# Attention scores of two heads in row groups of 64, value products next to the scores, and two moves in the gated recurrence

## The chip, the core and the metric

The kernel runs on one core of one Trainium2 chip. TensorE (PE) multiplies matrices; "PEld" is its weight load. VectorE (DVE), ScalarE (ACT) and GpSimd (POOL) do the elementwise work, SyncE (SP) issues the DMAs. The metric is the device time of one execution in microseconds; the median of several runs is given.

## The reference, cut to what matters

One layer of a hybrid streaming encoder: 1024 tokens of width 1024. A normed input is projected to a gated recurrence with four heads of 128 (branch a), a band attention with eight heads of 64 (branch b), and two gates; the branches are merged, then follow a feed-forward part and a last gated addition. The change lies in the two token mixers:

```python
def band_attention(q, k, v, qn_g, kn_g, rel_bias):
    # each chunk of 64 tokens attends to itself and the previous 8 chunks
    qh = head_rms(q, qn_g); kh = head_rms(k, kn_g)
    scores = einsum('bnqhd,bnkhd->bnhqk', qc, kb) * 64 ** -0.5
    probs = softmax(where(valid, scores + bias, -1e30))
    return einsum('bnhqk,bnkhd->bnqhd', probs, vb)

# recurrence, per chunk and head: qt, kt, it are q, k and value, b the summed log decay
    o = (qt * exp(b)) @ state + attn @ it
    state = exp(b_last) * state + (kt * exp(b_last - b)).T @ it
# then o = head_rms(o, onorm_g) * silu(g)
```

## The kernel before, in words

Weights and activations are split into a high and a low part in a rounded 32-bit format (fp32r); a product of two split numbers is three matmuls, high by high, high by low and low by high. Everything that must keep its order is chained by hand: each matmul (`mul`, L84) and each transpose (`tr`, L87) in the order in which the code issues it, so too the DMAs on SP and the operations that go through the wrappers `self.V`, `self.A` and `self.G` (shown as L55). Operations called on `nc.scalar` or `nc.gpsimd` directly are placed by a scheduler. PSUM tiles (`pm`) come from a pool of single banks of 128 x 512.

**Recurrence** (`hgrn_mix`, L558 on; about 372 to 536.8 us). For each of four heads, levels m = 1, 2, 4 to 64 build the scores within blocks of 128 tokens; then the keys are transposed in two halves (copied by ACT, L625), and eight blocks follow one another: a state product `pk`, the two products of the output `po`, an update of the state on DVE. A finished half's squares and its power are made (ACT L652, POOL L653 and L654); its scaling `hgrn_gate` (ACT L663) and its transposed output `hgrn_out` come later, among the levels of the next head. Each `yield` hands over to the "fill", here `attn_in`: the projection of q and k for the attention, in pieces of matmuls with weights that POOL (`wl`, L130) and ACT (`wh`, L124) split. `attn_in` squares and sums each block's q and k (power on POOL, L729 and L730), scales them on DVE and stores them with two strided DMAs, each value twice.

**Attention** (`attention`, L877 on; 536.8 to 703 us). Four pairs of heads times eight query blocks of 128 are 32 steps, and two more to drain; the second pair lies between 579.78 and 619.64 us. A query block sees up to five key blocks. For step n the code issues: the scores of head 0; the transposes of the next step's q and k (`attn_stack`: four of 128 x 128, since each head's q and k lie there twice, one copy above the other); the scores of head 1; one piece of feed work (two in the first three steps); the transposed probabilities of step n−1 (`attn_pt`, ten transposes in a full step, and the reciprocal sums spread over 64 columns); the value products of step n−2 (`attn_pv`, the two heads in the two column halves of the array); another piece of feed. Feed are matmuls of branch a and of gates, three per piece. ACT stores the query as [high; low] on 128 rows and the keys as high and remainder (`k1`, `k2`, two slots each), each key twice; so one head's scores are two matmuls over 128 rows for each of one or two groups of key blocks (`attn_scores`). DVE makes the low parts (`scalar_tensor_tensor`), adds the bias and takes the row minimum of the negated scores; ACT takes the exponential.

Of the kernel before, what the change touches and what calls it, by code (L numbers as in the profile page):

```python
# [11 lines left out]
F32R = mybir.dt.float32r  # L12
U32 = mybir.dt.uint32
AF = mybir.ActivationFunctionType
ALU = mybir.AluOpType
AX = mybir.AxisListType

P = 128
# [24 lines left out]
def f32(ap):  # L43
    return ap.bitcast(F32)
# [13 lines left out]
class Trunk:  # L58
# [493 lines left out]
    def hgrn_mix(self, h):  # L552
# [20 lines left out]
        while m < P:  # L573
            nb = T // m
            qv = q[:, :].rearrange("p (j two m) -> p j two m", two=2, m=m)
            kv = kt[:, :].rearrange("p (j two m) -> p j two m", two=2, m=m)
            per = 64 // m
            ps = sums(2) if m == 1 else self.mm()
            for c in range(8):
                if 1 < m < 32:  # L580
                    some = 16 // m
                    for j in range(4):
                        b = c * per + j * some
                        self.mul(
                            ps[32 * j:32 * j + 32, 16 * c:16 * c + 16], kt[:, c * P + 32 * j:c * P + 32 * j + 32],
                            qv[:, b:b + some, 1, :], start=True, stop=True)
                elif m >= 32:
                    for j in range(per):
                        self.mul(ps[2 * m * j:2 * m * j + m, c * m:c * m + m], kv[:, c * per + j, 0, :], qv[:, c * per + j, 1, :], start=True, stop=True)
            tv = cur.rearrange("p (j two) -> p j two", two=2)  # L590
            self.V.tensor_tensor(qv[:, :, 1, :], qv[:, :, 1, :], tv[:, :, 0:1].to_broadcast([P, nb // 2, m]), ALU.mult)
            self.V.tensor_tensor(kv[:, :, 0, :], kv[:, :, 0, :], tv[:, :, 1:2].to_broadcast([P, nb // 2, m]), ALU.mult)
            nxt = tt[:, at_col:at_col + nb // 2]
            at_col += nb // 2
            self.V.tensor_tensor(nxt, tv[:, :, 0], tv[:, :, 1], ALU.mult)
            av = at[:, :].rearrange("p (c j two m) -> p c j two m", c=8, two=2, m=m)[:, :, :, 1, :]
            if 1 < m < 32:
                some = 16 // m
                for j in range(4):
                    rows, b = slice(32 * j, 32 * j + 32), j * some  # L600
                    mk = self.masks[rows, LEVELS.index(m), 16 * j:16 * j + 16].rearrange("p (j m) -> p j m", m=m).unsqueeze(1).to_broadcast([32, 8, some, m])
                    self.V.copy_predicated(av[rows, :, b:b + some, :], mk, ps[rows, :P].rearrange("p (c j m) -> p c j m", c=8, m=m))
            elif m == 1:
                mk = self.masks[:, LEVELS.index(m), :].rearrange("p (j m) -> p j m", m=m).unsqueeze(1).to_broadcast([P, 8, per, m])
                self.V.copy_predicated(av, mk, ps[:, :].rearrange("p (c j m) -> p c j m", c=8, m=m))
            else:
                for j in range(per):
                    rows = slice(2 * m * j, 2 * m * j + m)
                    (self.V.tensor_copy if j == 0 else nc.scalar.copy)(av[rows, :, j, :], ps[rows, :8 * m].rearrange("p (c m) -> p c m", m=m))
            cur = nxt  # L610
            yield 1900 if m == 1 else 2400 if m < 32 else 1400 if m == 32 else 2000
            if m == 1:
                yield from self.hgrn_out()
            if m == 2:
                self.hgrn_gate()
            if m == 4:
                yield from self.hgrn_out()
            m *= 2

        ktok = self.slot()  # L620
        for i in range(2):
            ps = self.mm()
            for c in range(4):
                self.tr(ps[:, c * P:c * P + P], kt[:, i * HALF + c * P:i * HALF + c * P + P], self.eye)
            nc.scalar.copy(ktok[:, i * HALF:i * HALF + HALF], ps)  # L625
            yield 600
        if self.oa[h] is None:
            self.oa[h] = self.slot()
        for c in range(8):
            cs = slice(c * P, c * P + P)  # L630
            if c % 4 == 0:
                po = self.mm()
            if c < 7:
                pk = self.mm()
                self.mul(pk[:, :P], ktok[:, cs], v[:, cs], start=True, stop=True)
            o = po[:, (c % 4) * P:(c % 4) * P + P]
            self.mul(o, at[:, cs], v[:, cs], start=True, stop=c == 0)
            if c:
                self.mul(o, q[:, cs], state, start=False, stop=True)
            if c == 0:  # L640
                self.V.tensor_copy(state, pk[:, :P])
            elif c < 7:
                self.V.scalar_tensor_tensor(state, state, cur[:, c:c + 1], pk[:, :P], ALU.mult, ALU.add)
            yield 450
            if c == 6:
# [59 lines left out]
        self.G.tensor_scalar(bt, bt, -1.0, None, ALU.mult)  # L705

    def attn_keys(self):
        self.k1 = [self.slot(F32R) for _ in range(2)]
        self.k2 = [self.slot(F32R) for _ in range(2)]

    def attn_values(self):
        self.v = [self.slot() for _ in range(4)]
# [3 lines left out]
    def attn_in(self):  # L716
# [15 lines left out]
        def scale():  # L732
            g, b, ps, ss, _ = late.pop(0)
            t = self.small(HALF, tag="qo")
            self.V.tensor_tensor(
                t[:, :].rearrange("p (a d) -> p a d", d=64), ps[:, :].rearrange("p (a d) -> p a d", d=64),
                ss[:, :].unsqueeze(2).to_broadcast([P, 8, 64]), ALU.mult)
            to = self.qd[g, b] = self.spill()
            for i in range(2):
                self.store(  # L740
                    to[:, :].rearrange("p (a two d) -> p a two d", two=2, d=64)[:, :, i, :], t[:, :].rearrange("p (a d) -> p a d", d=64))

        for g in range(2):
            gates = iter(range(len(CHUNKS) - len(PLAIN) + g, len(CHUNKS), 2))
# [51 lines left out]

    def attn_load(self, pair, b):
        qk = self.qk[pair, b] = self.small(HALF, tag="qk")
        self.load(qk, self.qd[pair // 2, b][:, pair % 2 * HALF:pair % 2 * HALF + HALF])

    def attn_stack(self, pair, b):

        qk = self.qk.pop((pair, b))
        ps = self.mm()
        for a in range(4):
            self.tr(ps[:, a * P:a * P + P], qk[:, a * P:a * P + P], self.eye)
        q = self.qs[pair, b] = self.small(256, F32R, tag="qs")
        c = slice(b % 4 * 256, b % 4 * 256 + 256)
        k1, k2 = self.k1[b // 4][:, c], self.k2[b // 4][:, c]
        gk = self.cols[:, C_GK:C_GK + 1]  # L810
        self.A.activation(k1, ps[:, 256:512], AF.Copy, scale=gk)
        self.A.activation(q, ps[:, 0:256], AF.Copy, scale=self.gq8[:, 0:1])
        yield
        self.V.scalar_tensor_tensor(k2, ps[:, 256:512], gk, f32(k1), ALU.mult, ALU.subtract)
        lo = q[64:128, :]
        self.V.scalar_tensor_tensor(lo, ps[64:128, 0:256], self.gq8[64:128, 0:1], f32(lo), ALU.mult, ALU.subtract)

    def attn_scores(self, pair, b, h):

        k0 = max(0, b - 4)  # L820
        nb = b + 1 - k0
        bias = self.bias[pair, h]
        q = self.qs[pair, b][:, h * P:h * P + P]
        s = self.small(640, tag="s")
        mn = self.small(2, tag="mx2")
        last = None
        for i in range(2):
            lo, hi = max(k0, 4 * i), min(b + 1, 4 * i + 4)
            if hi <= lo:
                continue  # L830
            ps = self.mm()[:, :(hi - lo) * P]
            for j, k in enumerate((self.k1[i], self.k2[i])):
                keys = k[:, :].rearrange("p (b two t) -> p b two t", two=2, t=P)[:, lo - 4 * i:hi - 4 * i, h, :]
                self.mul(ps, q, keys, start=j == 0, stop=j == 1)
            c = slice((lo - k0) * P, (hi - k0) * P)
            e = slice(640 + (lo - b - 1) * P, 640 + (hi - b - 1) * P)
            init = 3.0e38 if last is None else last
            self.V.tensor_tensor_reduce(s[:, c], ps, bias[:, e], 1.0, init, ALU.add, ALU.min, mn[:, i:i + 1])
            last = mn[:, i:i + 1]
        return s[:, :nb * P], last  # L840

# [30 lines left out]
    def attention(self, fill):  # L872
# [1 line left out]
        steps = [(p, b) for p in range(4) for b in range(8)]  # L874
        whole = len(steps)
        feed = chain(fill, self.branch_a())
        sc, dens, pts = {}, {}, {}  # L877

        def stack(n):
            if n >= whole:  # L880
# [3 lines left out]
                self.bias_load(p + 1, b == 5)  # L884
            return self.attn_stack(p, b)

        def scores(n, h):
            if n < whole:
                sc[n, h] = self.attn_scores(*steps[n], h)

        def exp(n, h):
            if n < whole:
# [4 lines left out]
        def norm(n):  # L897
            if 0 <= n < whole:
                self.V.reciprocal(dens[n], dens[n])
# [15 lines left out]
        for n in range(whole + 2):  # L915
            if n < whole and steps[n][1] == 0:
                self.ob.append(self.slot())
            norm(n - 1)
            scores(n, 0)
            st = stack(n + 1)  # L920
            next(st, None)
# [2 lines left out]
            exp(n, 0)  # L924
            drain(st)
            scores(n, 1)
            for _ in range(2 if n < 3 else 1):
                next(feed, None)
            pt(n - 1, 0)
            pt(n - 1, 1)  # L930
# [9 lines left out]
                self.scale()  # L940
            if n > 3:
                next(item, None)
            next(feed, None)
        drain(feed)

    def branch_src(self):
# [1013 lines left out]
```

## Time and profile before

| | us |
|---|---|
| median of 3 runs | 1590.02 |
| lowest and highest | 1587.98 and 1591.01 |
| the profiled execution's own time | 1587.8 |
| its span, first to last instruction | 1586.0 |
| PE busy in it | 1554.9 (98%) |
| DVE busy | 1165.6 (73%) |
| POOL busy | 724.0 (46%) |
| ACT busy | 613.0 (39%) |

The mean clock granted to TensorE was 0.998 of full speed. Busy times of matmuls overlap, since a matmul starts while the one before it still drains; from one start to the next is what a matmul takes of PE's time. A row of a timeline gives the start and the length in us, the engine, line and operation, the tiles written and read (buffer numbers left out), the array's part used (rows x columns), and how many like it follow one another; in square brackets stands the idle time before it and the engine that ended it.

### The profile page before, as it was taken

How to read it: one execution, taken by the hardware profiler on the slowest of the kernel's cores; microseconds unless marked ns; L12 is line 12 of the kernel's file. 1: busy time of each engine (PE TensorE's matmuls, PEld its weight loads, DVE VectorE, ACT ScalarE, POOL GpSimd, SP SyncE). 2: the span in 40 equal slices, each digit the busy share in tenths (PEclk: the TensorE clock that was granted, in tenths of full speed). 3: DMA queues.
4: the chain of work that ended last, by engine and by line, in shares of the span. 5: the costliest groups of instructions: out<-in, count | busy, mean ns of one | idle time of the engine just before them, and what ended most of it. 6: DMA issues, size and time to landing. Idle time of an engine off the chain costs nothing. (4 is left out here: it accounts for less than half of the span.)

```text
span 1586.0 us, 22842 instructions
## 1 busy us (share of the span) xinstructions
PE 1554.9 (98%) x8708; PEld 1275.0 (80%) x8708; DVE 1165.6 (73%) x1582; ACT 613.0 (39%) x1033; POOL 724.0 (46%) x459
## 2 busy tenths in 40 slices
PE   8999999999989999999999999999999999999998
PEld 6888877887767788888888788888888887888887
DVE  8748787847887577766888888888888757438653
ACT  6332233332323566652567222222222235337321
POOL 4213342244545711106213677777777756446420
PEclk9999999999999999999999999999999999999999
DMA  5326666461542765444345323333233287655521
GB/s 192 133 94 227 241 208 219 160 221 66 167 135 55 238 201 171 171 157 175 107 157 185 118 100 109 101 108 104 100 100 100 73 302 272 215 178 178 196 73 53
DMA packets 125085, 244.22 MB, mean 154 GB/s; under 512 B 42800, under 2 KB 51504, under 8 KB 124208
## 3 DMA queue, kind: packets, MB, share of 16 engines
q1 hardware_dynamic: 124832, 242.75, 44.6%
q8 instruction: 68, 1.11, 0.3%
q14 instruction: 41, 0.34, 0.1%
q10 hardware_dynamic: 144, 0.02, 0.0%
HBM read 166.97 MB, written 75.76 MB: 153 GB/s over the span
## 5 line engine op out<-in xcount | busy, mean ns | idle before, releaser
L84 PE MATMUL pm<-s,whi 128*128 128x512 f32 x1808 | 563.9, 393 | 2.7 <-DVE t L55 2.4
L84 PE MATMUL pm<-s,wh 128*128 128x512 f32 (+1 forms) x1496 | 464.4, 392 | 2.2 <-DVE s L55 2.0
L84 PEld LDWEIGHTS pm<-s,whi 128*128 128x128 f32 x1808 | 339.3, 188 | 81.0 <-DVE t L55 3.2
L84 PE MATMUL pm<-s,wlo 128*128 128x512 f32 x904 | 355.2, 393 | 0.0
L130 POOL TENSOR_TENSOR wl<-wr,wh 128x1024 fp32r<-128x1024 f32 (+2 forms) x114 | 225.1, 1989 | 247.5 <-ACT wh L124 245.0
L55 DVE TENSOR_TENSOR s<-s,s 128x512 f32<-128x512 f32 (+3 forms) x249 | 285.6, 1168 | 61.1 <-ACT s L55 42.6
L84 PEld LDWEIGHTS pm<-s,wh 128*128 128x128 f32 x1496 | 275.8, 188 | 61.6 <-issue 5.5
L84 PE MATMUL pm<-s,wl 128*128 128x512 f32 (+1 forms) x748 | 290.4, 388 | 1.3 <-POOL wl L130 1.3
L84 PEld LDWEIGHTS pm<-s,wlo 128*128 128x128 f32 x904 | 169.8, 188 | 39.3 <-DVE wlo L55 0.2
L55 DVE TENSOR_TENSOR t<-pm,t 128x512 f32<-128x512 f32 x166 | 114.0, 687 | 93.0 <-PE pm L84 86.3
L84 PE MATMUL pm<-wh,s 128*128 128x512 f32 x512 | 171.1, 401 | 5.3 <-ACT wh L124 5.3
L84 PEld LDWEIGHTS pm<-s,wl 128*128 128x128 f32 x748 | 140.8, 188 | 30.8 <-POOL wl L130 1.7
L124 ACT CAST wh<-wr 128x1024 fp32r<-128x1024 f32 (+1 forms) x91 | 91.6, 1008 | 179.8 <-PE pm L84 90.0
L55 POOL TENSOR_TENSOR wlo<-wr,whi 128x512 fp32r<-128x512 f32 (+1 forms) x62 | 115.9, 1877 | 84.1 <-ACT whi L55 82.7
L55 DVE TENSOR_TENSOR s<-pm,s 128x512 f32<-128x512 f32 x117 | 77.4, 687 | 90.9 <-PE pm L84 87.5
L84 PEld LDWEIGHTS pm<-wh,s 128*128 128x128 f32 x512 | 97.1, 190 | 25.3 <-ACT wh L124 5.3
L55 POOL TENSOR_TENSOR s<-s,t 128x512 f32<-128x512 f32 x44 | 76.9, 1748 | 88.6 <-ACT t L55 88.6
L55 ACT CAST whi<-q 128x512 fp32r<-128x512 f32 (+1 forms) x63 | 47.8, 759 | 151.0 <-DVE q L55 130.5
L84 PE MATMUL pm<-wl,s 128*128 128x512 f32 x256 | 100.9, 394 | 1.2 <-POOL wl L130 1.2
L55 ACT CAST s<-s 128x1024 fp32r<-128x1024 f32 x76 | 75.7, 1009 | 46.5 <-DMA s<-d 23.4
L55 POOL TENSOR_TENSOR wlo<-q,whi 128x512 fp32r<-128x512 f32 x41 | 70.5, 1718 | 14.4 <-ACT whi L55 14.4
L55 ACT ACTIVATE t<-s 128x512 f32<-128x512 f32 x44 | 27.9, 634 | 123.0 <-DVE s L55 119.5
(148 smaller groups left out, 1970.9 us busy)
## 6 DMA issues: line engine op xcount, KB each, us to landing
s<-d SPq DMA_DIRECT2D x79, 512.0 KB, 5.6
d<-s SPq DMA_DIRECT2D x123, 256.0 KB, 2.9
wr<-d SPq DMA_DIRECT2D x28, 512.0 KB, 3.6
d<-t SPq DMA_DIRECT2D x54, 256.0 KB, 2.6
wr<-in_sg SPq DMA_DIRECT2D x22, 512.0 KB, 4.0
wr<-in_su SPq DMA_DIRECT2D x22, 512.0 KB, 4.3
d<-m SPq DMA_DIRECT2D x40, 256.0 KB, 3.7
m<-d SPq DMA_DIRECT2D x32, 256.0 KB, 3.4
```

Source lines behind the costliest of these rows:

```text
L55: return lambda *a, **k: self.trunk.order(op(*a, **k), self.key)
L84: return self.order(self.nc.tensor.matmul(*a, **k))
L124: self.nc.scalar.copy(hi[:, c], raw[:, c])
L130: rest.tensor_tensor(lo[:, c], raw[:, c], f32(hi[:, c]), ALU.subtract)
```

## The change

1. **Scores.** q and k are stored once, in one contiguous store per block, and loaded 256 columns wide. `attn_stack` makes two transposes: head 0's 64 features land on rows 0 to 63, head 1's on rows 64 to 127. Query and keys are split into high and low for both heads at once, with the keys in one slot each for `k1` and `k2`. A new function `attn_products` issues for each group of key blocks (up to four, or three and two when there are five) three products per head (high·high, high·low, low·high), head 0 on rows 0 to 63 and head 1 on rows 64 to 127 alternating, each head in a PSUM bank of its own; a step with five key blocks takes four banks.
2. **Order.** `products(n)` stands at the start of step n, right behind the value products of the step before; all feed pieces of the step stand in its middle.
3. **Recurrence, gating.** `hgrn_gate` comes behind level 4 instead of level 2, the second `hgrn_out` behind level 16 instead of level 4.
4. **Recurrence, state.** The first state product and its copy to `state` come right behind the transposes of the second half of the keys, without a fill piece between; they need the first half only.

```diff
-            if m == 2:
+            if m == 4:
                 self.hgrn_gate()
-            if m == 4:
+            if m == 16:
                 yield from self.hgrn_out()
...
             nc.scalar.copy(ktok[:, i * HALF:i * HALF + HALF], ps)
+            if i:
+                pk = self.mm()
+                self.mul(pk[:, :P], ktok[:, :P], v[:, :P], start=True, stop=True)
+                self.V.tensor_copy(state, pk[:, :P])
             yield 600
...
-            if c < 7:
+            if 0 < c < 7:
                 pk = self.mm()
...
-            if c == 0:
-                self.V.tensor_copy(state, pk[:, :P])
-            elif c < 7:
+            if 0 < c < 7:
                 self.V.scalar_tensor_tensor(state, state, cur[:, c:c + 1], pk[:, :P], ALU.mult, ALU.add)
...
-        self.k1 = [self.slot(F32R) for _ in range(2)]
-        self.k2 = [self.slot(F32R) for _ in range(2)]
+        self.k1, self.k2 = self.slot(F32R), self.slot(F32R)
...
-            for i in range(2):
-                self.store(
-                    to[:, :].rearrange("p (a two d) -> p a two d", two=2, d=64)[:, :, i, :], t[:, :].rearrange("p (a d) -> p a d", d=64))
+            self.store(to[:, :HALF], t)
...
-        for a in range(4):
+        for a in range(2):
             self.tr(ps[:, a * P:a * P + P], qk[:, a * P:a * P + P], self.eye)
...
-        self.A.activation(k1, ps[:, 256:512], AF.Copy, scale=gk)
-        self.A.activation(q, ps[:, 0:256], AF.Copy, scale=self.gq8[:, 0:1])
+        self.A.activation(k1, ps[:, P:2 * P], AF.Copy, scale=gk)
+        self.A.activation(q1, ps[:, :P], AF.Copy, scale=gq)
         yield
-        self.V.scalar_tensor_tensor(k2, ps[:, 256:512], gk, f32(k1), ALU.mult, ALU.subtract)
-        lo = q[64:128, :]
-        self.V.scalar_tensor_tensor(lo, ps[64:128, 0:256], self.gq8[64:128, 0:1], f32(lo), ALU.mult, ALU.subtract)
-
-    def attn_scores(self, pair, b, h):
+        self.V.scalar_tensor_tensor(k2, ps[:, P:2 * P], gk, f32(k1), ALU.mult, ALU.subtract)
+        self.V.scalar_tensor_tensor(q2, ps[:, :P], gq, f32(q1), ALU.mult, ALU.subtract)
+
+    def attn_products(self, pair, b):
...
+        q = self.qs.pop((pair, b))
+        cuts = [0, nb] if nb < 5 else [0, 3, nb]
+        parts = [[], []]
+        for lo, hi in zip(cuts, cuts[1:]):
+            c = slice((k0 + lo) * P, (k0 + hi) * P)
+            ps = [self.mm()[:, :(hi - lo) * P] for _ in range(2)]
+            for j, (qs, ks) in enumerate(((q[:, :P], self.k1), (q[:, :P], self.k2), (q[:, P:], self.k1))):
+                for h in range(2):
+                    rows = slice(64 * h, 64 * h + 64)
+                    self.mul(ps[h], qs[rows, :], ks[rows, c], start=j == 0, stop=j == 2)
+            for h in range(2):
+                parts[h].append((lo, hi, ps[h]))
+        return nb, parts
...
-            ps = self.mm()[:, :(hi - lo) * P]
-            for j, k in enumerate((self.k1[i], self.k2[i])):
-                keys = k[:, :].rearrange("p (b two t) -> p b two t", two=2, t=P)[:, lo - 4 * i:hi - 4 * i, h, :]
-                self.mul(ps, q, keys, start=j == 0, stop=j == 1)
...
             norm(n - 1)
+            products(n)
             scores(n, 0)
...
-            for _ in range(2 if n < 3 else 1):
+            for _ in range(3 if n < 3 else 2):
                 next(feed, None)
...
-            next(feed, None)
```

PE, a step with four key blocks in the second pair, before: the row of the value products' end (tile `m` by `s`, 64 wide), the feed piece (tiles `wh`, `wl`), then the scores of head 0, four transposes, the scores of head 1 and the feed again.

```order
L84 MATMUL pm_5685<-m_5611,s_4944 64x128 x2
L84 MATMUL pm_5669<-s_4596,wh_4915 128x512
L84 MATMUL pm_5669<-s_4597,wh_4915 128x512
L84 MATMUL pm_5669<-s_4596,wl_4914 128x512
L84 MATMUL pm_5699<-s_4860,m_5654 128x512
L84 MATMUL pm_5699<-s_4862,m_5654 128x512
L87 MATMUL pm_5703<-eye,m_5446 128x128 x4
L84 MATMUL pm_5719<-s_4860,m_5654 128x512
L84 MATMUL pm_5719<-s_4862,m_5654 128x512
L84 MATMUL pm_5669<-s_4702,wh_4915 128x512
```

The same place now (`s_4848` is k1, `s_4849` is k2, the two `pm` are the two heads' banks):

```order
L84 MATMUL pm_5113<-m_5053,s_4927 64x128 x2
L84 MATMUL pm_5118<-s_4848,m_5076 128x512
L84 MATMUL pm_5119<-s_4848,m_5076 128x512
L84 MATMUL pm_5118<-s_4849,m_5076 128x512
L84 MATMUL pm_5119<-s_4849,m_5076 128x512
L84 MATMUL pm_5118<-s_4848,m_5076 128x512
L84 MATMUL pm_5119<-s_4848,m_5076 128x512
L87 MATMUL pm_5129<-eye,m_4925 128x128 x2
L84 MATMUL pm_5094<-s_4692,wh_4878 128x512
L84 MATMUL pm_5094<-s_4693,wh_4878 128x512
```

The feed piece has gone from between the value products and the scores; six products in one piece stand where four in two pieces stood.

PE in the recurrence, end of head 0's transposes (tiles `eye`), as the difference between the two kernels; `s_2621` holds the values, `s_3172` the transposed keys:

```order
 L87 MATMUL pm_3173<-eye,s_2708 128x128 x4
 L87 MATMUL pm_3179<-eye,s_2708 128x128 x4
+L84 MATMUL pm_3185<-s_2621,s_3172 128x128
 L84 MATMUL pm_3131<-wh_2614,s_256 128x512
 L84 MATMUL pm_3131<-wl_2613,s_256 128x512
```

The first state product is now ahead of the fill piece that stood between it and the transposes.

POOL between heads 1 and 2, before: powers of two q/k blocks (L729, L730), two weight pieces (L130) and the power of a finished half (L653, L654).

```order
L729 TENSOR_TENSOR m_3805<-m_3805,mhalf 128x8
L730 TENSOR_SCALAR m_3805<-m_3805,m_464 128x8
L130 TENSOR_TENSOR wl_3730<-wr_3732,wh_3731 128x256 x4
L729 TENSOR_TENSOR m_3808<-m_3808,mhalf 128x8
L730 TENSOR_SCALAR m_3808<-m_3808,m_464 128x8
L130 TENSOR_TENSOR wl_3794<-wr_3796,wh_3795 128x256 x4
L653 TENSOR_SCALAR m_3849<-m_3849 128x4
L654 TENSOR_TENSOR m_3849<-m_3849,mhalf 128x4
```

And now:

```order
L130 TENSOR_TENSOR wl_3727<-wr_3729,wh_3728 128x256 x4
L130 TENSOR_TENSOR wl_3788<-wr_3790,wh_3789 128x256 x4
L730 TENSOR_TENSOR m_3799<-m_3799,mhalf 128x8
L731 TENSOR_SCALAR m_3799<-m_3799,m_464 128x8
L730 TENSOR_TENSOR m_3802<-m_3802,mhalf 128x8
L731 TENSOR_SCALAR m_3802<-m_3802,m_464 128x8
L655 TENSOR_SCALAR m_3843<-m_3843 128x4
L656 TENSOR_TENSOR m_3843<-m_3843,mhalf 128x4
```

Both weight pieces have moved ahead of the powers of the q/k blocks; the half's power is last in both.

More of the change, by code (lines that the diff above doesn't have):

```diff
@@ L798, in attn_load @@
         qk = self.qk[pair, b] = self.small(HALF, tag="qk")
-        self.load(qk, self.qd[pair // 2, b][:, pair % 2 * HALF:pair % 2 * HALF + HALF])
+        self.load(qk[:, :256], self.qd[pair // 2, b][:, pair % 2 * 256:pair % 2 * 256 + 256])
     def attn_stack(self, pair, b):
@@ L804, in attn_stack, with attn_scores @@
         ps = self.mm()
-        for a in range(4):
+        for a in range(2):
             self.tr(ps[:, a * P:a * P + P], qk[:, a * P:a * P + P], self.eye)
         q = self.qs[pair, b] = self.small(256, F32R, tag="qs")
-        c = slice(b % 4 * 256, b % 4 * 256 + 256)
-        k1, k2 = self.k1[b // 4][:, c], self.k2[b // 4][:, c]
-        gk = self.cols[:, C_GK:C_GK + 1]
-        self.A.activation(k1, ps[:, 256:512], AF.Copy, scale=gk)
-        self.A.activation(q, ps[:, 0:256], AF.Copy, scale=self.gq8[:, 0:1])
+        c = slice(b * P, b * P + P)
+        k1, k2, q1, q2 = self.k1[:, c], self.k2[:, c], q[:, :P], q[:, P:]
+        gk, gq = self.cols[:, C_GK:C_GK + 1], self.gq8[:, 0:1]
+        self.A.activation(k1, ps[:, P:2 * P], AF.Copy, scale=gk)
+        self.A.activation(q1, ps[:, :P], AF.Copy, scale=gq)
         yield
-        self.V.scalar_tensor_tensor(k2, ps[:, 256:512], gk, f32(k1), ALU.mult, ALU.subtract)
-        lo = q[64:128, :]
-        self.V.scalar_tensor_tensor(lo, ps[64:128, 0:256], self.gq8[64:128, 0:1], f32(lo), ALU.mult, ALU.subtract)
-    def attn_scores(self, pair, b, h):
+        self.V.scalar_tensor_tensor(k2, ps[:, P:2 * P], gk, f32(k1), ALU.mult, ALU.subtract)
+        self.V.scalar_tensor_tensor(q2, ps[:, :P], gq, f32(q1), ALU.mult, ALU.subtract)
+    def attn_products(self, pair, b):
         k0 = max(0, b - 4)
         nb = b + 1 - k0
+        q = self.qs.pop((pair, b))
[11 more added lines that the diff above has]
+        return nb, parts
+    def attn_scores(self, pair, nb, parts, h):
         bias = self.bias[pair, h]
-        q = self.qs[pair, b][:, h * P:h * P + P]
         s = self.small(640, tag="s")
@@ L826, in attn_scores @@
         last = None
[L827 to L830, printed above, removed]
-            ps = self.mm()[:, :(hi - lo) * P]
-            for j, k in enumerate((self.k1[i], self.k2[i])):
-                keys = k[:, :].rearrange("p (b two t) -> p b two t", two=2, t=P)[:, lo - 4 * i:hi - 4 * i, h, :]
-                self.mul(ps, q, keys, start=j == 0, stop=j == 1)
-            c = slice((lo - k0) * P, (hi - k0) * P)
-            e = slice(640 + (lo - b - 1) * P, 640 + (hi - b - 1) * P)
+        for i, (lo, hi, ps) in enumerate(parts[h]):
+            e = slice(640 + (lo - nb) * P, 640 + (hi - nb) * P)
             init = 3.0e38 if last is None else last
-            self.V.tensor_tensor_reduce(s[:, c], ps, bias[:, e], 1.0, init, ALU.add, ALU.min, mn[:, i:i + 1])
+            self.V.tensor_tensor_reduce(s[:, lo * P:hi * P], ps, bias[:, e], 1.0, init, ALU.add, ALU.min, mn[:, i:i + 1])
             last = mn[:, i:i + 1]
@@ L876, in attention @@
         feed = chain(fill, self.branch_a())
-        sc, dens, pts = {}, {}, {}
+        sc, dens, pts, prods = {}, {}, {}, {}
         def stack(n):
@@ L885, in stack, with products @@
             return self.attn_stack(p, b)
+        def products(n):
+            if n < whole:
+                prods[n] = self.attn_products(*steps[n])
         def scores(n, h):
             if n < whole:
-                sc[n, h] = self.attn_scores(*steps[n], h)
+                sc[n, h] = self.attn_scores(steps[n][0], *prods[n], h)
         def exp(n, h):
```

## The prediction

> **What bounds the kernel now.** I read the page first, then the waits of TensorE (PE), then busy time by stage, then a timeline of one attention step. The page's span and its row of busy times (busy us, share of the span, instructions):
>
> ```profile
> span 1586.0 us, 22842 instructions
> PE 1554.9 (98%) x8708; PEld 1275.0 (80%) x8708; DVE 1165.6 (73%) x1582; ACT 613.0 (39%) x1033; POOL 724.0 (46%) x459
> ```
>
> PE is the bound: 31 us of the span is left idle. Four of its waits lie where the change works (us in total, times, longest):
>
> ```profile
> PE pm L84 <- ACT m L663: 4.8, 2, 4.1
> PE pm L84 <- DVE s L55: 4.5, 8, 1.3
> PE pm L84 <- POOL wl L130: 2.5, 3, 1.3
> PE pm L84 <- DVE state L55: 1.7, 2, 0.9
> ```
>
> Busy time in the gated recurrence (372 to 536.8), in the attention, and in the attention's second head pair alone (window: length, busy us of PE, weight loads, DVE, ACT, POOL, granted clock, DMA share, GB/s):
>
> ```profile
> 372.00:536.80 164.80, 155.49 (x1716) 125.63 (x1715) 119.72 (x237) 54.30 (x152) 87.09 (x91) 0.99 0.38 112
> 536.80:703.00 166.20, 164.19 (x1378) 138.94 (x1377) 128.14 (x384) 113.78 (x273) 34.34 (x37) 1.00 0.55 179
> 579.78:619.64 39.86, 39.86 (x341) 33.96 (x340) 31.30 (x96) 27.30 (x67) 6.40 (x6) 1.00 0.55 182
> ```
>
> In the second pair PE works for 39.86 of 39.86 us. So a PE instruction taken out of the attention is time gained, as long as DVE, 31.30 us busy, stays below. Its last step, PE's timeline (start, us until the last one's end, instructions grouped):
>
> ```profile
> 613.69 0.86 PE L84 MATMUL pm<-s,m 128*128 128x128 f32 x4
> 614.38 0.60 PE L87 MATMUL pm<-eye,m 128*128 128x128 f32 x4
> 614.74 0.93 PE L84 MATMUL pm<-s,m 128*128 128x128 f32 x4
> 615.51 0.62 PE L84 MATMUL pm<-s,wh 128*128 128x512 f32 x2
> 615.97 0.39 PE L84 MATMUL pm<-s,wl 128*128 128x512 f32 x1
> 616.20 1.25 PE L87 MATMUL pm<-eye,m 128*128 128x128 f32 x10
> 617.38 0.44 PE L84 MATMUL pm<-eye,m 128*64 128x128 f32 x4
> 617.65 1.26 PE L84 MATMUL pm<-m,s 128*64 128x128 f32 x20
> 618.84 0.73 PE L84 MATMUL pm<-s,wh 128*128 128x512 f32 x2
> 619.40 0.40 PE L84 MATMUL pm<-s,wl 128*128 128x512 f32 x1
> 619.64 0.33 PE L84 MATMUL pm<-s,m 128*128 128x128 f32 x2
> ```
>
> The busy times overlap; what counts is start to start. The step takes 619.64 − 613.69 = 5.95 us: scores of head 0 (.69), four transposes (.36), scores of head 1 (.77), three feed products of 512 columns (.69, so .23 each), ten transposes (1.18), 24 half-width matmuls (1.46), three feed products (.80).
>
> **The scores.** The 16 score blocks of the second pair, from one's start to the next instruction's (window: length, PE busy); first, last and sum:
>
> ```profile
> 579.78:579.95 0.17, 0.17 (x3) 1.00 0.00 0
> ...
> 614.74:615.51 0.77, 0.77 (x8) 1.00 0.00 0
> ...
> sum 8.09, PE 8.09; mean PE 0.51
> ```
>
> Removed: 8.09 × 4 pairs = 32.4 us. Removed too: two of four transposes in each of 32 steps, at about .10 (.36/4 = .09, 1.18/10 = .118): 6.4 us.
>
> Added: per cut three products for each head, the two heads in different halves of the array's rows. If both run at once, a pair costs what one costs: 512 columns .23, in proportion .17 for 384 and .115 for 256, and about .11 for 128, where the next weights set the pace as in the transposes. Eight steps: one block 3 × .11 = .33; two 3 × .115 = .345; three 3 × .17 = .51; four 3 × .23 = .69; then four steps of five blocks, 3 × .17 + 3 × .115 = .858 each, 3.43. Sum 5.31, × 4 = 21.2 us. It is 144 pairs in all (3, 3, 3, 3 and 4 × 6, times four).
>
> No row shows two row halves at once. The nearest are two column halves, in a timeline of 0.1 us:
>
> ```profile
> 617.65 0.28 PE L84 MATMUL pm<-m,s 128*64 128x128 f32 x2
> ```
>
> and their group in the second pair (busy us, mean ns of one, idle before):
>
> ```profile
> L84 PE MATMUL pm<-m,s 128*64 128x128 f32 x120 | 7.9, 273 | 0.0
> ```
>
> Two that take .273 each are over within .28, so the second started some .007 behind the first. Bounds for the row halves: full overlap, 21.2, and none, 42.5; I take the first, the row it is nearest to.
>
> **The array's mode.** The order on PE becomes: products (row halves), transposes and feed (whole array), transposes, sums and value products (column halves), then the next products. That is three changes of shape a step where there were two. From 616.20 to 619.64 the trace shows a round trip, whole to columns to whole: 3.44 us, against 10 × .10 + 12 column pairs × .11 + 3 × .23 = 3.01 without changes, so .43 at that reckoning and .35 if a transpose is .109. I take .18 for one change: 32 × .18 = 5.8 us, bounds 0 and .35 × 32 = 11.2. The Trainium skill, page "TensorEngine Tiling (Array Packing)", Key Properties, says that changing the tiling mode, and not merely the tile, drains the TensorE. By that rule products directly behind value products pay such a drain and the term stands; were it false here, the term would be 0 and the sum 5.8 lower. The round trip agrees with the rule, and no row shows column to row.
>
> The feed products keep their number and their 512 columns; three of six change places: nothing. They ask for their weights 1.18 + 1.46 = 2.6 us earlier in the step; if those came late it would cost such a wait as the three of PE for POOL wl above, 2.5/3 = .8 each, but in the second pair PE never waited for them.
>
> **DVE.** Its rows in the second pair (busy us, mean ns, idle before):
>
> ```profile
> L55 DVE SCALAR_TENSOR_TENSOR m<-pm,gq,m 64x256 fp32r<-64x256 f32 x8 | 3.9, 491 | 0.1
> L55 DVE SCALAR_TENSOR_TENSOR s<-pm,cols,s 128x256 fp32r<-128x256 f32 x8 | 3.9, 484 | 3.8 <-ACT m L55 3.7
> ...
> L55 DVE TENSOR_TENSOR s<-pm,m 128x128 f32<-128x128 f32 x8 | 2.3, 291 | 1.3 <-PE pm L84 1.2
> ```
>
> Both subtractions become 128 wide: by the last row .29 instead of .49 and .48, 8 × .39 = 3.1 us less of 31.3. PE's pair falls by 11.8/4 = 2.95 to 36.9, so DVE is 28.2/36.9 = 76% busy. The next products wait for this step's subtractions and for free banks, the reductions of head 1 among them; ahead of them on PE stand the six feed products, ten transposes and 24 half-width matmuls, 1.4 + 1.2 + 1.5 = 4.1 us, and all of DVE's work of a step is 28.2/8 = 3.5. That hides it; without the cover the cost is the rival below.
>
> **DMA.** Stores and loads of q and k (KB each, us to landing):
>
> ```profile
> d<-m SPq DMA_DIRECT2D x40, 256.0 KB, 3.7
> m<-d SPq DMA_DIRECT2D x32, 256.0 KB, 3.4
> ```
>
> Loads halve and the paired strided stores become one. SP issues a load five steps (some 25 us) ahead of its use: nothing gained.
>
> **The recurrence.** The first state product is now straight behind the second half's transposes and needs ACT's copy of the first half. Transposes and copies of heads 1 and 3, and where PE went on:
>
> ```profile
> 426.16 1.03 PE L87 MATMUL pm<-eye,s 128*128 128x128 f32 x8
> 426.95 0.48 PE L84 MATMUL pm<-wh,s 128*128 128x512 f32 x1
> 427.20 0.59 ACT L625 COPY s<-pm 128x512 f32<-128x512 f32 x1
> 516.62 1.03 PE L87 MATMUL pm<-eye,s 128*128 128x128 f32 x8
> 517.31 1.08 ACT L625 COPY s<-pm 128x512 f32<-128x512 f32 x2 [3.77 <-PE pm L87]
> ```
>
> PE could go on .79 after the first transpose: at 426.95 and 517.41. The first copies end at 427.79 and 517.31 + .54 = 517.85. So a new wait of .84 where ACT is held up and .44 where not. Behind it on PE stand feed products that were its cover. Three heads at .44 and one at .84: +2.2 us. Removed: PE's wait for DVE's state, 1.7. Net +.5, bounds −1.7 and 4 × .84 − 1.7 = +1.7.
>
> The gating of a finished head moves from behind level 2 to behind level 4, the second output from behind level 4 to behind 16. The longest wait above, 4.1, sits there:
>
> ```profile
> 447.74 3.71 POOL L130 TENSOR_TENSOR wl<-wr,wh 128x256 fp32r<-128x256 f32 x4
> 451.87 1.04 POOL L654 TENSOR_TENSOR m<-m,mhalf 128x4 f32<-128x4 f32 x1
> 452.94 1.14 ACT L663 ACTIVATE m<-pm,m 128x128 f32<-128x128 f32 x4 [9.48 <-POOL m L654]
> 454.13 1.03 PE L84 MATMUL pm<-s,s 128*32 128x16 f32 x64 [4.13 <-ACT m L663]
> ```
>
> PE needs a bank that ACT's gating frees, ACT needs POOL's power (L654), and POOL had weights to split first. In the new order POOL does both weight pieces, then both powers of the q/k blocks, then this one: the same work stands ahead of it, so 4.1 stays. Taken at 0; bounds −4.1 if level 4 gets another bank, +4 if the q/k blocks, now scaled behind 3.71 us more of POOL work, hold their banks that much longer.
>
> **Sum.** −32.4 − 6.4 + 21.2 + 5.8 + .5 = −11.3 against the profiled execution's 1587.8: 1576.5. The median is 1590.0, 2.2 above that, so 1578.7. With the switch at 0 it is 1572.9, at its other bound 1584.1: own range 1572 to 1584.5.
>
> **Rivals.** *The row halves run one behind the other* (slower). For: no row shows two at once. Against: the column halves. The 144 pairs cost 42.5, +21.3: +10.0, 1600. It decides from the point where the second head starts over 11.3/144 = .078 us behind the first, where columns show .007.
>
> *Part overlap*: streams share a path, or weight loads queue, and a pair costs 1.5 times a single: +10.6, −.7, 1589. For: 12 column pairs take 1.46/12 = .122, more than a transpose. At 1.2 times, −7.1, 1583. The Trainium skill, "TensorE: Matmul & The Clock Gate", Measured speedup vs the span model, gives 3.07 times for four row tiles of 32 rows at 512 columns, by which four cost 1.30 singles; as an estimate from that page a pair at that price gives −4.9, 1585. No run here shows it.
>
> *PE freed, but DVE or banks late*: a step of five blocks asks for four banks at once. DVE s above waits 4.5/8 = .56 a time; at half the 16 such steps +4.5, −6.8: 1583; at all, 1588. Against: no wait at all in the second pair, and DVE at 76%.
>
> **How the numbers follow.** Forecast .60; one behind the other .13; part overlap .14, half of it near 1589; DVE or banks .13. A difference within 0.2% (3.2 us) can't be told from none. Faster: .60 + .13 + .03 of part overlap = .76; same .11, the rest of it; slower .13. The range 1571 to 1590 leaves out the slower rival and little more.
>
> **What would show it.** In the second pair: PE busy falls to about 36.9 us and stays without waits; the products of a five-block step take .86 between starts, plus a switch of .18 ahead of them; DVE near 28. A five-block product group of 1.7 us is the first rival, 1.3 the second; waits of PE for DVE s in every step the third. In the recurrence: no wait for DVE state, four short ones for ACT's copy. A step of 6 us or more refutes the forecast; so does a gain that comes from elsewhere.

## The result, and the profile after

The changed kernel takes 1573.81 us (median of 5 runs, 1572.32 to 1576.26) where the kernel before took 1589.47 (5 runs, 1587.98 to 1591.01): a ratio of 0.9901, 95% interval 0.989 to 0.9911, so 15.7 us faster. Two more measurements of the same two kernels, the first and the ninth run below, gave 13.4 and 15.0 us. The profiled execution took 1576.26 us, the longest of its five; that of the kernel before, 1587.8, is a little below the shortest of its five. The two traces therefore differ by 11.5 us only.

The page of the changed kernel, and PE's waits in it (us in total, times, longest):

```profile
span 1574.5 us, 22862 instructions
PE 1545.8 (98%) x8740; PEld 1261.9 (80%) x8740; DVE 1152.8 (73%) x1582; ACT 605.0 (38%) x1033; POOL 725.2 (46%) x459
```

```profile
PE pm L84 <- DVE s L55: 6.5, 7, 2.7
...
PE pm L84 <- POOL wl L130: 2.8, 4, 1.4
PE pm L84 <- ACT s L625: 1.4, 4, 0.7
PE pm L84 <- DVE state L55: 0.7, 2, 0.5
```

The waits for ACT's gating (4.8) are gone, those for DVE have grown from 4.5 to 6.5, those for DVE's state have fallen from 1.7 to .7, four for ACT's copy of the keys are new. By stage, with the same columns as before (recurrence, attention, second head pair):

```profile
372.00:537.03 165.03, 157.27 (x1718) 126.12 (x1716) 119.55 (x241) 54.51 (x152) 86.66 (x93) 0.99 0.28 93
537.03:691.00 153.97, 153.30 (x1411) 125.64 (x1411) 112.88 (x384) 106.28 (x273) 32.92 (x36) 1.00 0.47 159
575.83:612.86 37.03, 37.03 (x350) 30.49 (x348) 27.21 (x95) 25.22 (x67) 6.42 (x6) 1.00 0.48 167
```

The second pair takes 37.03 us instead of 39.86, PE still works all of it, and DVE has 27.21 us of work there: the gain is PE's own time. The last step of that pair, PE's timeline:

```profile
607.48 1.14 PE L84 MATMUL pm<-s,m 64*128 64x384 f32 x12
608.55 0.44 PE L87 MATMUL pm<-eye,m 128*128 128x128 f32 x2
608.75 0.71 PE L84 MATMUL pm<-s,wh 128*128 128x512 f32 x2
609.29 0.40 PE L84 MATMUL pm<-s,wl 128*128 128x512 f32 x1
609.53 0.62 PE L84 MATMUL pm<-s,wh 128*128 128x512 f32 x2
609.99 0.39 PE L84 MATMUL pm<-s,wl 128*128 128x512 f32 x1
610.22 1.25 PE L87 MATMUL pm<-eye,m 128*128 128x128 f32 x10
611.40 0.44 PE L84 MATMUL pm<-eye,m 128*64 128x128 f32 x4
611.67 1.26 PE L84 MATMUL pm<-m,s 128*64 128x128 f32 x20
612.86 0.55 PE L84 MATMUL pm<-s,m 64*128 64x128 f32 x6
```

From start to start: twelve products 1.07, two transposes .20, six feed products 1.47, then as before 1.18 and 1.46; 5.38 us instead of 5.95. The products' row shows the array's part as 64 x 128.

For the stages three rows of PE's timeline serve as marks: the recurrence's first sums, the first score, and the last long group of value products. In the kernel before and in the changed one:

```profile
356.08 1.10 PE L84 MATMUL pm<-m,onesr 128*128 128x512 f32 x4
536.80 0.42 PE L84 MATMUL pm<-s,m 128*128 128x128 f32 x2
700.39 2.35 PE L84 MATMUL pm<-m,s 128*64 128x128 f32 x40
```

```profile
357.12 1.10 PE L84 MATMUL pm<-m,onesr 128*128 128x512 f32 x4
537.03 0.55 PE L84 MATMUL pm<-s,m 64*128 64x128 f32 x6
688.29 2.35 PE L84 MATMUL pm<-m,s 128*64 128x128 f32 x40
```

The attention (second mark to third) fell from 163.59 to 151.26 us, by 12.33. The recurrence (first to second) fell from 180.72 to 179.91, by .8. What comes ahead of the first mark took 1.0 us longer, what comes behind the third .6 (885.6 and 886.2 us to the end of the span); the change does not touch either.

### The profile page after: what moved, and what is told of

Its sections match the earlier page's. It is cut to its first block, busy times and chain, and to the rows that moved or that the text cites. A ratio compares the mean times of both kernels' runs of the same rounds, so it can differ in the third digit from the quotient of the medians.

```text
span 1574.5 us, 22862 instructions
## 1 busy us (share of the span) xinstructions
PE 1545.8 (98%) x8740; PEld 1261.9 (80%) x8740; DVE 1152.8 (73%) x1582; ACT 605.0 (38%) x1033; POOL 725.2 (46%) x459
## 5 line engine op out<-in xcount | busy, mean ns | idle before, releaser
L130 POOL TENSOR_TENSOR wl<-wr,wh 128x1024 fp32r<-128x1024 f32 (+2 forms) x114 | 224.4, 1982 | 248.1 <-ACT wh L124 247.7
L84 PEld LDWEIGHTS pm<-s,wlo 128*128 128x128 f32 x904 | 169.7, 188 | 39.5 <-DVE wlo L55 0.4
```

Source lines behind the costliest of these rows:

```text
L84: return self.order(self.nc.tensor.matmul(*a, **k))
L130: rest.tensor_tensor(lo[:, c], raw[:, c], f32(hi[:, c]), ALU.subtract)
```

## The experiments

All medians stand beside runs of the kernel before on the same chip, 1589.3 to 1589.8 in each group.

| run | what | median (range) | ratio to before, 95% | recurrence | attention |
|---|---|---|---|---|---|
| 1 | changed kernel again | 1576.39 (1575.28 to 1577.06) | 0.9915 (0.9901 to 0.9928) | 180.36 | 151.29 |
| 2 | head 0's products, then head 1's | 1577.12 (1573.41 to 1577.87) | 0.9917 (0.9903 to 0.9931) | 180.10 | 151.93 |
| 3 | a feed piece between | 1580.86 (1579.78 to 1581.37) | 0.9944 (0.9931 to 0.9956) | 179.18 | 156.93 |
| 4 | kernel before, feed moved | 1588.99 (1585.66 to 1590.76) | 0.9994 (0.9985 to 1.0003) | 180.51 | 162.67 |
| 5 | both heads in one row half | 1596.46 (1594.64 to 1596.52) | 1.0039 (1.0027 to 1.0052) | 179.83 | 171.77 |
| 6 | head 1's products left out | 1575.66 (1573.42 to 1576.47) | 0.9909 (0.9896 to 0.9923) | 179.31 | 153.04 |
| 7 | gating not moved | 1573.31 (1572.13 to 1573.70) | 0.9895 (0.988 to 0.991) | 177.96 | 151.14 |
| 8 | state product not moved | 1574.06 (1573.48 to 1575.46) | 0.9903 (0.9889 to 0.9916) | 178.58 | 151.47 |
| 9 | changed kernel, third time | 1574.27 (1573.16 to 1575.95) | 0.9902 (0.9887 to 0.9916) | 179.34 | 151.04 |
| 10 | run 7 again | 1573.83 (1572.83 to 1575.42) | 0.9896 (0.9879 to 0.9912) | 179.77 | 151.60 |
| 11 | attention's part alone | 1572.42 (1572.04 to 1573.43) | 0.9890 (0.9875 to 0.9905) | 177.28 | 151.76 |
| 12 | run 7, weight pieces in turns | 1575.48 (1573.67 to 1577.51) | 0.9909 (0.9894 to 0.9923) | 177.27 | 152.70 |

The last two columns are differences of the marks, in us of the one traced execution. Runs 1 to 4, 5 to 8 and 9 to 12 ran on one chip each.

### 1. The changed kernel again

> The changed kernel itself, once more with a profile beside the kernel before. The median gain was 15.7 us, the two profiled executions differ by only 11.5. Theory A (attention alone): the attention is 12.3 us shorter in the trace, everything else is the spread of single executions; then a second trace has the same attention to 0.1 us, and the gain of the medians is again 14 to 16 us with the difference spread over stages that the change does not touch. Theory B (a second gain in the recurrence that the one trace missed): the stretch from 372 us to the attention's first score is 2 us or more shorter than in the first trace of the changed kernel.

The attention took 151.29 us, within .03 of the first trace. The recurrence took 180.36, longer and not shorter. The medians differ by 13.4 this time, a little less than the 14 to 16 of theory A. So the attention is a fixed amount, theory B falls, and what lies beyond 12.3 us varies from one measurement to the next.

A part of that variation can be seen here. PE's idle time in the recurrence was less than in the first trace (7.2 us instead of 7.8), but behind a wait of 2.6 us the clock stayed at half for longer (window: length, PE busy, granted clock, DMA share, GB/s; from 450 to 452 it was .82):

```profile
452.00:454.00 2.00, 2.00 (x67) 0.50 0.00 0
454.00:456.00 2.00, 2.00 (x6) 0.50 0.38 139
456.00:458.00 2.00, 2.00 (x6) 0.50 0.00 0
```

That is 2 x .18 + 6 x .50 = 3.4 us of clock missing, where the first trace misses 1.7 (its rows stand under run 8).

### 2. One head's products after the other's

```diff
-            for j, (qs, ks) in enumerate(((q[:, :P], self.k1), (q[:, :P], self.k2), (q[:, P:], self.k1))):
-                for h in range(2):
+            for h in range(2):
+                for j, (qs, ks) in enumerate(((q[:, :P], self.k1), (q[:, :P], self.k2), (q[:, P:], self.k1))):
```

> All three products of head 0, then all three of head 1, instead of alternating; nothing else. Theory A (the gain hangs on neighbours in different row halves running at once): only the third product of head 0 and the first of head 1 overlap, so a group costs five widths instead of three; a five-block step's products take about 1.06 + 2 x 0.17 + 2 x 0.115 = 1.63 us instead of 1.06, the sum over the attention is 2/3 of 21.2 = 14 us more, and the median is about 1588, nearly that of the kernel before. Rival B (the row halves overlap whatever their order, because the matmuls of a half queue up by themselves): within 2 us of the changed kernel.

Theory A fell. The products' group in a five-block step, and a timeline of .15 us at the start of one:

```profile
608.63 1.14 PE L84 MATMUL pm<-s,m 64*128 64x384 f32 x12
609.70 0.44 PE L87 MATMUL pm<-eye,m 128*128 128x128 f32 x2
```

```profile
593.36 0.45 PE L84 MATMUL pm<-s,m 64*128 64x384 f32 x2
```

1.07 us, as with alternating heads, and two matmuls of .44 are over within .45, so the second started .01 behind the first. The timeline does not name the heads, but two matmuls in one row half do not overlap like this (run 5); so the second is taken to be the other head's, although the code issues two more of the first head ahead of it. The alternating order in the code is not what makes them overlap. The median is .7 above run 1's and the attention .6 longer, as rival B has it.

### 3. A feed piece between value products and products

```diff
-            for _ in range(3 if n < 3 else 2):
+            for _ in range(2 if n < 3 else 1):
                 next(feed, None)
...
+            next(feed, None)
```

> One feed piece put back between the value products and the products, as in the kernel before: the array changes shape four times a step instead of three (columns, whole, row halves, whole). Theory A (a change costs about 0.1 us, as the traces' starts now show: 0.20 instead of 0.10 between the last value product and the first product): +0.1 x 32 = 3.2 us, median 1577. Rival B (0.18 a change, as predicted): +5.8, 1579.6. Rival C (changes cost nothing, the place of the products only matters for DVE's cover): within 1 us.

The attention is 5.67 us longer than the changed kernel's 151.26: 5.67/32 = .177 for one more change of shape a step. The median rose by 4.5. Rival B, the size of the prediction, holds; the .1 that I had read from one gap was too small. A step shows where the rest is:

```profile
592.10 0.73 PE L84 MATMUL pm<-s,wh 128*128 128x512 f32 x2
592.66 0.40 PE L84 MATMUL pm<-s,wl 128*128 128x512 f32 x1
592.99 1.13 PE L84 MATMUL pm<-s,m 64*128 64x384 f32 x12
```

Three feed products between two changes of shape take .89 (592.10 to 592.99) where three whole-array products between whole-array work took .69: .20, about what the step lost. The Trainium skill, "TensorEngine Tiling (Array Packing)", Key Properties, has the rule that changing the tiling mode drains the TensorE; its price is in these rows.

### 4. The kernel before with its feed moved

```diff
-            for _ in range(2 if n < 3 else 1):
+            for _ in range(3 if n < 3 else 2):
                 next(feed, None)
...
-            next(feed, None)
```

> The kernel before with one edit: both feed pieces in the middle of the step, so that the old whole-array scores stand directly behind the value products. Theory A (the gain is in the row halves): columns to whole is paid once either way, one interruption fewer of the feed gives about 0.28 us a head pair, so -1 us and up to -1.2 more for the waits at the attention's start: 1587.5 to 1589 where the kernel before has 1589.5. Rival B (the new place of the scores is what brings the gain): 1582 or less.

Attention 162.67, .92 less than before; the median .8 less, interval across 1. Theory A holds: the new place of the scores by itself is worth about 1 us, and .5 of that is PE's idle time in the attention (2.0 us before, 1.5 here).

### 5. Both heads in one row half

```diff
-                    rows = slice(64 * h, 64 * h + 64)
+                    rows = slice(0, 64)
```

> Both heads' products on rows 0 to 63 (head 1's scores are then computed from head 0's query and keys), the number and width of the matmuls unchanged. The serial run showed that the heads overlap in any order; here they can't. Theory A (the overlap of the two row halves is what the change lives on): every pair costs two widths, a five-block step's products take about 1.06 + 0.86 = 1.92 us, the attention is 21 us longer, median about 1597, slower than the kernel before. Rival B (PE is not what sets the attention's time any more, so the overlap is worth less): less than +10, 1586 or below.

```profile
597.46 2.02 PE L84 MATMUL pm<-s,m 64*128 64x384 f32 x12
599.41 0.44 PE L87 MATMUL pm<-eye,m 128*128 128x128 f32 x2
```

The same twelve matmuls take 1.95 us instead of 1.07. The attention is 171.77 us, 20.5 more (20.5/144 = .142 a pair, .15 by widths; the wait of .7 in the attention's first steps is gone in this trace, so the products cost 21.2 more), and the kernel is slower than before, 1.0039 (1.0027 to 1.0052). Theory A holds, and this is the prediction's slower rival made real: without the overlap the change loses.

### 6. Head 1's products left out

```diff
-            ps = [self.mm()[:, :(hi - lo) * P] for _ in range(2)]
+            ps = [self.mm()[:, :(hi - lo) * P]] * 2
...
-                for h in range(2):
+                for h in range(1):
                     rows = slice(64 * h, 64 * h + 64)
```

> Head 1's products left out: both heads' softmax reads head 0's scores, from one bank per cut instead of two. Theory A (the second head is free, it starts 3 to 10 ns behind the first): 144 x 0.004 = 0.6 us less, median within 1.5 us of the changed kernel. Rival B (a pair costs something, in PE, in weight loads or in banks): each 0.01 us a pair is 1.4 us; at 1.2 widths a pair -4.2 us.

```profile
592.12 1.13 PE L84 MATMUL pm<-s,m 64*128 64x384 f32 x6
593.18 0.44 PE L87 MATMUL pm<-eye,m 128*128 128x128 f32 x2
```

Six matmuls take 1.06, twelve 1.07, and the median is within the spread of the changed kernel (1573.8 to 1576.4): the second head is free. Theory A holds, the rival of part overlap falls. By the Trainium skill's "TensorE: Matmul & The Clock Gate", Measured speedup vs the span model, four row tiles reach 3.07 times; two halves here reach two times, as near as the rows can tell. The attention's 153.04 is 1.8 more than the changed kernel's, not less. A wait of 1.2 us, up to 546.3, instead of .7 adds .5, and the clock missing behind it 1.7 (2 x .30 + 2 x .50 in the windows below, .1 in the next). Against that the products themselves took .5 less (27.4 instead of 28.0 us from start to start over the whole attention), close to the .6 of theory A. The two windows (length, PE busy, granted clock, DMA share, GB/s):

```profile
546.00:548.00 2.00, 1.66 (x5) 0.70 0.71 281
548.00:550.00 2.00, 2.00 (x8) 0.50 0.05 16
```

### 7 and 10. The gating back behind level 2

```diff
-            if m == 4:
+            if m == 2:
                 self.hgrn_gate()
-            if m == 16:
+            if m == 4:
                 yield from self.hgrn_out()
```

> The changed kernel with the gating and the second output back behind levels 2 and 4. Theory A (the move shortens PE's longest wait there from 4.1 to 2.7, since another bank comes free first): that wait is 4.1 again and the one of 0.6 ahead of it is back, the smaller ones at 499.9 and 504.4 shrink by 0.9 together: +1 to +2 us between the start of the recurrence and the attention's first score, median +1 to +2. Rival B (as predicted, POOL's queue sets the time in either order): 0 to 0.3 us in that stretch.

> The changed kernel with gating and second output back behind levels 2 and 4, a second time, beside the changed kernel on one chip. Theory A (the gating's move costs 2 us when the early state product is there): stretch of the recurrence 178.0, 2 us below the changed kernel, median 1.5 to 2.5 below. Rival B (the difference of the first look was the spread between calls): the same within 0.5 us in that stretch.

The seventh run had a recurrence of 177.96 us, the tenth, the same kernel, 179.77. Its waits for DVE in the two traces, 372 to 537:

```profile
PE pm L84 <- DVE s L55: 3.8, 6, 2.1
```

```profile
PE pm L84 <- DVE s L55: 5.4, 7, 2.7
```

In one execution the long wait ahead of level 4 of the third head was absent, in the other it was 2.7 us. PE's idle time in the whole stretch is 5.9 and 7.7 us, which accounts for the difference of the two. Theory A of the seventh run (+1 to +2) fell, and theory A of the tenth (2 us less) with it: beside the changed kernel the medians are 1573.83 and 1574.27, the stretches 179.77 and 179.34. The gating's move is worth nothing that these runs can show.

### 8. The first state product back behind a fill piece

The edit is the reverse of the diff's `if i:` and `0 < c < 7`.

> The changed kernel with the first state product back behind a fill piece. Theory A (one wait is exchanged for another: two waits for the state, 1.7 us, against four for ACT's copy and two for the state, 2.1): the stretch from the recurrence's start to the attention's first score changes by -0.5 to +0.3 us, the median not measurably. Rival B (the early product lets the whole chain of states run ahead): +1 us or more without it.

178.58 us in the recurrence, .8 to 1.8 less than the three traces of the changed kernel, the median 1574.06 within their spread. The waits for ACT's copy are gone as theory A has it, but three for the state take 2.1 us, not 1.7, and one of 1.6 for ACT's gating is new. The waits come to 8.0 us, the changed kernel's to 7.7. Still the stretch came out shorter than the bounds of theory A, for a reason that neither theory had: the clock. In the changed kernel PE waits 2.7 us ahead of level 4 of the third head and then works at half clock; here it waits 2.0 and does not (changed kernel, then this run):

```profile
452.00:454.00 2.00, 1.30 (x65) 0.79 0.17 64
454.00:456.00 2.00, 2.00 (x6) 0.50 0.34 131
456.00:458.00 2.00, 2.00 (x23) 0.86 0.03 8
```

```profile
452.00:454.00 2.00, 0.45 (x2) 1.00 0.31 122
454.00:456.00 2.00, 1.51 (x68) 1.00 0.07 26
456.00:458.00 2.00, 2.00 (x10) 1.00 0.34 131
```

The clock missing in the first three rows is about 1.7 us of work: 2 x .21 + 2 x .50 + 2 x .14 = 1.7.

### 9 and 11. The changed kernel, and the attention's part alone

> The changed kernel once more, as the measure for the three runs beside it: 1574 to 1576.5, the stretch from the recurrence's first sums to the attention's first score 179.9 to 180.4 us, the attention 153.4 us from its first score to its last value product.

> The attention's part of the change alone: both edits of the recurrence undone. Theory A (each of the two edits alone shortens the long wait ahead of a finished head's bank, by 2 to 3 us, and both together give most of it back): without both the stretch is again the 180.7 us of the kernel before, the longest wait 4.1 us on ACT's gating, the attention 153.4: 0.3 to 0.8 us above the changed kernel. Rival B (both edits are losses and the attention's lighter stores shorten the recurrence): 178 us or less in that stretch.

The changed kernel's median, 1574.27, is as expected; its recurrence, 179.34, is .6 below the expected range, and its attention within .3 of the first two traces.

Theory A of the eleventh run fell: without both edits the recurrence took 177.28 us, not 180.7. But that rival B named the right side does not show its cause. PE's waits there sum to 7.3 us, as in the ninth run (4.6 + 1.4 + .8 + .5 = 7.3):

```profile
PE pm L84 <- DVE s L55: 5.4, 6, 2.1
PE pm L84 <- DVE state L55: 0.9, 1, 0.9
PE pm L84 <- POOL wl L130: 0.8, 2, 0.6
PE pm L84 <- ACT m L663: 0.2, 1, 0.2
```

Without its waits the stretch took 170.0 us here, and 172.0 in the ninth run, where the clock fell behind the wait of 2.6; here it did not. The median, 1572.42, is the lowest of all, 1.9 below the changed kernel beside it, but their ranges still touch (1573.43 and 1573.16) and the ratios' intervals overlap. What can be said: the attention's part carries the gain alone, and the two edits of the recurrence add nothing to it that these runs can show.

### 12. Weight pieces in turns

On the kernel of run 7, for the recurrence only:

```diff
-                self.cuts = 4
+                self.cuts, self.by_turns = 4, True
...
-                self.cuts = 1
+                self.cuts, self.by_turns = 1, False
```

> As the run without the gating's move, and the low parts of every second weight piece of the recurrence made on DVE instead of POOL. Theory A (DVE's queue is what PE waits for there now, 3.8 us in six waits against 0.6 for POOL): the 0.6 goes, DVE's waits grow: 0 to +2 us against the run without the move. Rival B (DVE is late because POOL's powers stand behind weight pieces): the wait of 2.1 shrinks and it is 1 to 2 us faster, the fastest of all.

The wait for weight pieces is gone, others of 1.0 to 1.4 us are new, the recurrence took 177.27 us, and in the attention's first steps PE waited 1.1 and 1.2 us where .7 stood. The wait of 2.1 that rival B wanted to shrink is 2.1 here too. The recurrence is shorter than in runs 7 and 10, against theory A; no clock is missing in it. The median is 1575.48, 1.7 above run 10: theory A's side, but the ranges overlap, so no difference is shown.

## Why the prediction was right, and where it was not

**The sum.** Against the profiled execution it said 1576.5; the profiled execution of the changed kernel took 1576.26. The measured terms of the attention are differences of the two traces, each summed over the attention's 32 steps from one PE instruction's start to the next one's, with PE's idle time kept apart:

| term | forecast | measured |
|---|---|---|
| old scores | −32.4 | −32.5 |
| row-half products with one more change of shape | 21.2 + 5.8 = 27.0 | 28.0 |
| two transposes fewer a step | −6.4 | 11.2 became 6.0: −5.2 |
| feed in one piece | 0 | 52.8 became 51.7: −1.1 |
| idle time, the waits of the attention's first steps | not named | 2.0 became .7: −1.3 |
| the rest of the attention | 0 | −.2 |
| attention in all | −11.8 | −12.3 |
| recurrence | +.5 | −.8, −.4 and −1.4 in three traces |

So that the attention came out within .5 us is in part luck: the products cost 1.0 more and the transposes saved 1.2 less than forecast, and the feed and the waits, which were taken at nothing, gave 2.4 back. That the whole execution came out within .3 us is luck too: the recurrence gave 1.3 us more than forecast, and the stages that the change does not touch took 1.6 us longer.

The waits in the fifth row (kernel before, then changed, from the first score on; the rest of the 2.0 are gaps too short to be listed):

```profile
PE pm L84 <- DVE s L55: 1.3, 1, 1.3
PE pm L87 <- DVE s L55: 0.6, 1, 0.6
```

```profile
PE pm L84 <- DVE s L55: 0.7, 1, 0.7
```

**Row halves at once** was right, and runs 5 and 6 show it from both sides: one row half costs 20.5 us more where the rival said 21.3, one head less gains nothing in the median. **The change of shape** at .18 was right to the hundredth (run 3). **DVE's cover** was right: no wait in the second pair. **The transposes** were mis-sized: four take .36 us and two .20, so two fewer save .16 a step and not .20.

**The recurrence** came out on the other side of nothing. The state product's exchange of waits came to +.4 (1.7 us became 1.4 + .7) where +.5 was forecast, but by two errors that cancel: ACT's copy costs 1.4 and not 2.2, and .7 of the waits for the state remain where none was to be left. The step that failed is "the same work stands ahead of it, so 4.1 stays. Taken at 0": the wait became 2.7 and its releaser DVE instead of ACT, and DVE itself had just waited for POOL's power of a q/k block:

```profile
450.11 0.69 DVE L55 TENSOR_TENSOR m<-pm,m 128x512 f32<-128x512 f32 x1 [1.35 <-POOL m L731]
452.69 0.83 PE L84 MATMUL pm<-s,s 128*32 128x16 f32 x64 [2.66 <-DVE s L55]
```

The bound of −4.1 held it. The gating's move is not what ended the wait of 4.1: run 11 leaves the gating where it was, and in its trace the longest wait is 2.1, on DVE, where both traces with the old attention (the kernel before and run 4) have 4.1. The attention's part alone is enough; by which way it acts on the recurrence stays open. What the step lacked besides is that a wait there can cost half the clock afterwards, 1.7 us more or twice that, and that it differs from one execution to the next of the same kernel (runs 7 and 10). These two things are nearly all that differs: the stretch of the recurrence, less PE's idle time and less the missing clock, is 180.7 − 9.3 − 1.7 = 169.7 us in the kernel before, 179.9 − 7.8 − 1.7 = 170.4 in the changed one, and lies between 169.6 and 170.7 in all 14 traces.

**From the profiled time to the median** is where the 4.9 us between 1578.7 and 1573.8 arise. I added the 2.2 by which the median before stood above its traced execution. The changed kernel's traced execution stood 2.5 above its median instead. In runs 1 and 9, the same kernel, the traced execution stood .1 above and 1.1 below. So that offset is a property of one execution, not of the kernel: 2.2 + 2.5 = 4.7 of the 4.9. What differs between executions is in part visible, the stretch ahead of the recurrence (355.6 to 357.9 us over the traces) and the clock behind waits; the rest stays open.

## What to carry to other kernels

Two matmuls of 64 contracted rows in the two row halves cost one here (twelve 1.07 us, six 1.06), alternating or one head after the other, so a product that was widened to 128 rows by storing data twice is worth undoing, if three such products instead of two still come out ahead after one change of the array's shape is paid. Count the blocks of equal shape in a step: each further change cost .18 us here, 5.7 us in 32 steps. A forecast for a median should not inherit the offset of the one execution that was traced.

## What the runs showed of the hardware that was not expected

The granted clock halves for about 3.4 us behind some of PE's waits (1.7 us of clock missing, at half), and for twice that in run 1: behind 4.1 us in the kernel before, 2.7 in the changed one, 2.6 in run 1, 2.1 at 423.7 in run 7, 1.2 in run 6. Behind 2.0 to 2.1 us in runs 8, 11 and 12 it did not; run 12's wait stands at the same place of the code as run 7's. So length alone does not decide. A long wait is not needed either: in run 9 the clock fell at 840 us (.52 up to 842) behind 16 products of one column, 1.84 us in all, and a wait of .26. Run 7:

```profile
422.00:424.00 2.00, 0.35 (x6) 1.00 0.00 0
424.00:426.00 2.00, 2.00 (x18) 0.77 0.00 0
426.00:428.00 2.00, 2.00 (x6) 0.50 0.00 0
```

The Trainium skill, "TensorE: Matmul & The Clock Gate", What's actually happening, gives a window of about 3.4 us that runs free of the kernel, and a return to half clock after an idle window. The stretches of 3.4 us here, and of twice that in run 1, agree with the window, and so does an outcome that differs between executions; that 1.2 us of waiting can be enough does not fit an idle window of 3.4 us, and the measurement decides.
